# Block 1's key, value and query products in other places, and expert routing written as two generators

## The chip, the cores and the metric

One core of a Trainium2 chip runs the kernel. The metric is the time of one execution on the device in microseconds (us), and lower is better. The engines are TensorE (PE in the profile, with its weight loads as PEld), VectorE (DVE), ScalarE (ACT), GpSimd (POOL) and SyncE (SP). Sixteen DMA engines move data; SP issues the plain loads and POOL issues the gathers.

## The reference

The kernel computes two layers of a bidirectional encoder over 256 tokens with 1024 features. Cut to what matters, a layer is:

```python
h = rms_norm(x, attn_norm)
qa, ka, va, qb, kb, vb, qc, kc, vc = split(h @ w_in)     # three groups of heads of 64
q, k = rope(rms_norm(q)), rope(rms_norm(k))
o = softmax(q k^T + mask) v                              # full, dilated and windowed heads
x = x + (concat(rms(oA), rms(oB), rms(oC)) * out_norm) @ w_out
h = rms_norm(x, ffn_norm)
s = (h @ wq) against keys                                # 8 heads x 2 halves x 128 keys
sv, si = top_k(s, 16); best, pos = top_k(sv[0] + sv[1], 16)
idx = si[0][pos] * 128 + si[1][pos]; gate = softmax(best)
act = gelu(h . u[idx]) * gate                            # 128 experts for each token
x = x + sum_k act_k * v[idx_k]
```

Each token so picks 8 x 16 = 128 experts of 16384. A row of `u` and the row of `v` beside it make 8 KB for one token.

## The kernel before, in words

The 256 tokens are two blocks of 128, block 0 and block 1, with one token on each of the 128 partitions. Everything is 32-bit float. The program is written out in full by Python generators: each generator issues instructions and yields, and the order in which they are stepped is the order of the instructions on every engine.

A layer has a short part before the gather and a long part with it.

**Before the gather.** Block 1's keys and values come from `proj_kv(l, 1)`, which takes its columns in three pieces (`KCH`): 512 columns of keys, 256 columns of keys and values, and 512 columns of values. The two key pieces are followed by `qk_rope`, some 30 VectorE instructions. `keys_t` transposes the keys. Then `attn(l, 0, filler)` runs block 0's attention through `chain_idle`, where four pairs of heads go through `scores`, `softmax`, `divide`, `values` (transposing the weights) and `pv`, and `product` and `add` apply W_out. `chain_idle` steps a generator `filler` at one place, to put TensorE work between two waits. Before the change the filler is the third piece of `proj_kv(l, 1)`, called `values1`; its eight products with 512 columns are all issued there. Then block 0's expert routing begins: `route` makes one item of one or two heads (`HEADS`), in the order query product (`rq`), copy (`q2`), key scores (`rs`), copy (`sS`), the search for the best sixteen on VectorE (`top16`), the expert numbers (`EF`, `EI`), and the gate. While head 0 is routed, `mixer_in` and `proj_q(l, 1)` (block 1's queries, sixteen products with 512 columns) are stepped beside it. When head 0's numbers are there, POOL's gathers may begin; head 1 is routed to its end before the loop over gathered rows.

**The loop.** There are 256 rows n for a layer, 128 for each block. Row n of the loop is one expert for each of 128 tokens: `fetch` gathers 128 x 8 KB (1 MB) by one indirect DMA on POOL's queue, `dots` multiplies and sums on VectorE, `weigh` makes a diagonal matrix on ScalarE (Gelu, times the gate, times the identity), and `gather_up` adds the row to two PSUM banks by TensorE. A row lives in one of 16 slabs of 8 KB per partition, which it shares with the weights in use (w_out and wq hold eight of them while block 1's attention and routing are still to come), so that eight rows are under way at a time at first.

Between rows the loop steps two lanes, `rq` (routing) and `bg` (block 1's query rotation, attention and `mixer_in`, later the next layer's first products). What a step issues is counted by `Meter`: for VectorE 0.15 us and one us for 960 columns of each instruction, for TensorE four us for 2400 columns. Each row adds `DVE_SHARE` = 1.05 and `PE_SHARE` = 0.75 us of credit, up to `SAVED`:

```python
dq, pq = min(dq + DVE_SHARE, SAVED), min(pq + PE_SHARE, SAVED)
while dq > -0.5 and pq > -1.5:
```

Routing takes a step only while `dq` is above 0, and `bg` only while `pq` is. A step that yields n is not taken up again before n rows later. A row's gather needs the expert numbers of its head (16 rows a head), so the loop forces routing when it is late:

```python
while routed() < min((n + 3) // 16 + 1, 16):
    if not rq.step():
        bg.step()
```

Block 1's routing is opened when block 0's routing and block 1's attention are both through, or at row 112. PSUM has two banks for the accumulators and six for all else (`NPS`); `take` and `give` count them.

Of the kernel before, what the change touches and what calls it, by code (L numbers as in the profile page):

```python
# [8 lines left out]
F32 = mybir.dt.float32  # L9
# [11 lines left out]
NPS = 6  # L21
DVE_SHARE = 1.05
PE_SHARE = 0.75
SAVED = 0.8
LEAD = 30
EPS = 1e-6
NKV = 1280
# [32 lines left out]
def tile_trunk(ctx: ExitStack, tc: tile.TileContext, x, wkv, wq_in, w_out, wq, keys, uv0, uv1,  # L60
               cons, qkg, sinks, gains, out):
    nc = tc.nc
# [104 lines left out]
    def take(n):  # L167
        while room[0] < n:
            yield 1
        room[0] -= n  # L170
# [182 lines left out]
    def attn(l, b, filler=None):  # L353
# [53 lines left out]
        def divide(g):  # L407
            P = PR[g]
            ls, es = SM[g]
            if es is not None:  # L410
                dve.tensor_tensor(out=ls, in0=ls, in1=es, op=OP.add)
            dve.reciprocal(ls, ls)
            if idle:
                dve.tensor_tensor(out=P, in0=P, in1=ls.unsqueeze(2).to_broadcast([128, 4, 256]), op=OP.mult)
            else:
                for j in range(4):
                    nc.scalar.activation(P[:, j, :], P[:, j, :], AF.Copy, scale=ls[:, j:j + 1])  # L417
# [14 lines left out]
        def pv(g):  # L432
            hds = []
            for i in range(2):
                kind, hd = pair_info(2 * g + i)
                hds += [(h % 2, 3 * kind + h // 2, vh, 2 * i + s) for s, (h, vh) in enumerate(hd)]
            lo = [a for a in hds if a[0] == 0]
            hi = [a for a in hds if a[0] == 1]
            for pair in zip(lo, hi):
                for t in range(2):  # L440
                    for o, mt, vh, j in pair:
                        pe.matmul(mix[mt // 4][o * 64:o * 64 + 64, mt % 4, :], V[:, t, vh * 64:(vh + 1) * 64],
                                         PTT[g][:, t, j, :], start=(t == 0), stop=(t == 1),
                                         skip_group_check=True)
# [29 lines left out]
        def product(g, z):  # L474

            m0, m1 = GROUPS[g]
            p = ps(f"wo{l}{b}{g}{z}")
            for m in range(m0, m1):
                pe.matmul(p, mT[:, m, :], w_o(l, m, z), start=(m == m0), stop=(m == m1 - 1))
            return p  # L480
# [40 lines left out]
        def chain_idle():  # L521
            scores(0)
            softmax(0)
            scores(1)
            softmax(1)
            divide(0)
            steps(filler, 4)
            rest(keys_t(l, 1, 4, 5))
            rest(filler)
            rest(values(0))  # L530
            scores(2)
            divide(1)
            softmax(2)
            pv(0)
            rest(values(1))
            scores(3)
            divide(2)
            softmax(3)
            pv(1)
            rest(values(2))  # L540
            leave(0)
            divide(3)
            p0 = [product(0, z) for z in range(2)]
            rest(norm_sum(0))
            for z in range(2):
                add(0, z, p0[z])
            pv(2)
            rest(values(3))
            leave(1)
            p1 = [product(1, 0)]  # L550
            rest(norm_sum(1))
            pv(3)
            leave(2)
            p1.append(product(1, 1))
            for z in range(2):
                add(1, z, p1[z])
            rest(norm_sum(2))
            for z in range(2):
                add(2, z, product(2, z))
# [24 lines left out]
        yield from transposes(H2T[l, b].rearrange("p k t -> p (k t)"), 8, ev, f"h2p{l}{b}")  # L584


    BEST, EF, EI, DOT, DONE, GATE, ACT = {}, {}, {}, {}, {}, {}, {}

    def route_alloc(l, b):
        BEST[l, b] = sp.tile([128, 8, 16], F32, tag="best", name=f"best{l}{b}")  # L590
# [18 lines left out]
            dve.max_index(out=idx[:, 8:16], in_max=val[:, 8:16], in_values=scr)  # L609
        yield 0  # L610

    def route(l, b, h0, n):

        nm = f"{l}{b}{h0}"
        yield from take(1)
        pq = ps(f"rq{nm}")
        for hh in range(n):
# [6 lines left out]
        give(1)  # L624
        nc.scalar.activation(q2[:, :n * 128], pq[:, :n * 128], AF.Copy)  # L625
        yield from take(2)
        sS = sp.tile([128, 2, 256], F32, tag="sS", name=f"sS{nm}", bufs=1)
        pk = [ps(f"rs{nm}{p}") for p in range(2)]
        for hh in range(n):
            for p in range(2):  # L630
# [3 lines left out]
        give(2)  # L634
        for p in range(2):
            nc.scalar.activation(sS[:, p, :n * 128], pk[p][:, :n * 128], AF.Copy, scale=RF[l, b][:, 0:1])  # L636
        yield 1
        val = sp.tile([128, 2, 2, 16], F32, tag="rval", name=f"rv{nm}")[:, :, :n]
        idx = sp.tile([128, 2, 2, 16], U32, tag="ridx", name=f"ri{nm}")[:, :, :n]
        scr = sp.tile([128, 2, 128], F32, tag="rscr", name=f"rscr{nm}", bufs=1)  # L640
# [60 lines left out]
        dve.reciprocal(s, s)  # L701
        dve.tensor_tensor(out=g, in0=g, in1=s.unsqueeze(2).to_broadcast([128, n, 16]), op=OP.mult)
        GATED.setdefault((l, b), set()).update(range(h0, h0 + n))
        yield 0

    GATED = {}
# [16 lines left out]

    def weigh(l, b, s):

        a = ACT[l, b][:, s:s + 1]
        nc.scalar.activation(a, DOT[l, b][:, s:s + 1], AF.Gelu)  # L727
        nc.scalar.activation(a, a, AF.Copy, scale=GATE[l, b].rearrange("p h k -> p (h k)")[:, s:s + 1])  # L728
        d = DG[l, b, s] = sp.tile([128, 128], F32, tag="dg", name=f"dg{l}{b}{s}", bufs=4)
        nc.scalar.activation(d, ident, AF.Copy, scale=a)  # L730
# [13 lines left out]

    def open_block(l, b):
        DOT[l, b] = sp.tile([128, 128], F32, tag="dot", name=f"dot{l}{b}")
        ACT[l, b] = sp.tile([128, 128], F32, tag="act", name=f"act{l}{b}")


    uv_rows = (uv0, uv1)  # L750
# [9 lines left out]
    def steps(gen, n):  # L760
        for _ in range(n):
            if next(gen, None) is None:
                return

    def rest(gen):
        for _ in gen:
            pass
# [63 lines left out]
    for l in range(L):  # L831
        if l:
            rest(norm_h(l, 1))
        load(w_out, WO, l, "wo", range(4))
        rest(proj_kv(l, 1, KCH[:2]))
        if l == 0:
            rest(queries_t(0, 0))
        rest(keys_t(l, 1, 0, 4))
        values1 = proj_kv(l, 1, KCH[2:])
        rest(attn(l, 0, values1))  # L840
        load(wq, WQ, l, "wq", range(4))
        open_block(l, 0)
        route_alloc(l, 0)
        rq = Lane(*[route(l, 0, *h) for h in HEADS])

        def routed():
            return sum(len(GATED.get((l, b), ())) for b in range(2))

        hm = mixer_in(l, 0)
        pq1 = proj_q(l, 1)  # L850
        while 0 not in DONE.get((l, 0), ()):
            rq.step()
            steps(hm, 1)
            steps(pq1, 1)
        rest(hm)
        fetch(l, 0, 0)
        rest(pq1)
        finish(rq, until=lambda: routed() > 1)
        bg = Lane(rope_q(l, 1), queries_t(l, 1), attn(l, 1), mixer_in(l, 1))
        dq = pq = 0.0  # L860
        for n in range(256):
            b, s = n // 128, n % 128
            if s == 0:
                ACC[l, b] = [bank(f"acc{z}", f"acc{l}{b}{z}") for z in range(2)]

            dq, pq = min(dq + DVE_SHARE, SAVED), min(pq + PE_SHARE, SAVED)
            while dq > -0.5 and pq > -1.5:
                d, p = dve.spent, pe.spent
                late = routed() < min((n + LEAD) // 16 + 1, 16)
                lanes = (rq, bg) if late or rq.spent < bg.spent else (bg, rq)  # L870
                moved = next((x for x in lanes if (dq if x is rq else pq) > 0 and x.step(n)), None)
                if moved is None:
                    break
                d, p = dve.spent - d, pe.spent - p
                dq, pq = dq - d, pq - p
                moved.spent = max(moved.spent + d + p, max(rq.spent, bg.spent) - 4)
            if (l, 1) not in BEST and not (bg.left or rq.left) or n == 112 and (l, 1) not in BEST:
                finish(bg, rq)
                route_alloc(l, 1)
                open_block(l, 1)  # L880
                rq = Lane(*[route(l, 1, *h) for h in HEADS])
            while routed() < min((n + 3) // 16 + 1, 16):
                if not rq.step():
                    bg.step()
            if n == 132 and l + 1 < L:
                finish(bg)
                load_small(l + 1)
                load(wkv, WKV, l + 1, "wkv", range(5))
                bg = Lane(rope_tables(l + 1), norm_h(l + 1, 0), proj_kv(l + 1, 0), keys_t(l + 1, 0, 0, 4),
                          keys_t(l + 1, 0, 4, 5), once(load, wq_in, WQI, l + 1, "wqi", range(4)),  # L890
                          once(load_late, l + 1), proj_q(l + 1, 0), rope_q(l + 1, 0), queries_t(l + 1, 0))
            if n:
                fetch(l, b, s)
            dots(l, b, s)
            if n == 129:
                settle(l, 0)
            weigh(l, b, s)
            gather_up(l, b, s)
        finish(bg)
        settle(l, 1)  # L900
# [92 lines left out]
```

## Time and profile before

| what | us |
|---|---|
| median of 3 runs | 1558.68 |
| lowest and highest run | 1555.74, 1562.99 |
| the profiled execution, its own time | 1560.36 |
| its span, first to last instruction | 1558.6 |
| TensorE busy in it | 1319.9 |
| VectorE busy | 1036.2 |
| ScalarE busy | 681.5 |
| POOL busy (issuing gathers) | 619.3 |

Times in the rows are microseconds from the start of the span unless ns stands beside them. A matmul of 32-bit floats shows as two instructions. L55 is the line of the meter's helper, so that many operations of TensorE and VectorE have that line, and the tiles' names tell them apart.

### The profile page before, as it was taken

The numbers are of one execution on the slowest core, as the hardware profiler recorded it, in microseconds if no ns is written. First come the engines' busy times: TensorE is split into PE (matmuls) and PEld (weight loads), VectorE is DVE, ScalarE is ACT, GpSimd is POOL, SyncE is SP. The second block draws the span as 40 slices with busy tenths as digits, with TensorE's granted clock in tenths as the row PEclk, the third lists the DMA queues.
The fourth block names the chain that finished last, engine by engine and source line by source line (L and its number), as shares of the span: only waits on it lengthen the run. The fifth ranks groups of instructions, "written<-read, shape, count | busy, mean of one in ns | idle before, by whom it ended". The sixth has DMA issues, their size and how long they took to land. (4 is left out here: it accounts for less than half of the span.)

```text
span 1558.6 us, 15351 instructions
## 1 busy us (share of the span) xinstructions
PE 1319.9 (85%) x3860; PEld 591.2 (38%) x3860; DVE 1036.2 (66%) x3014; ACT 681.5 (44%) x2056; POOL 619.3 (40%) x516
## 2 busy tenths in 40 slices
PE   8896898998868898889878968989998788887777
PEld 4453353443323344433324534444333333332222
DVE  5667868685658777666536587786756767785444
ACT  1323657443434444444323236565434454444333
POOL 0004444555434443423410044545455455555551
PEclk9898999999998999999988989999999999999999
DMA  9308999999999999899991099999999999999996
GB/s 375 156 1 354 420 405 378 395 420 421 419 422 420 421 421 420 343 420 421 422 411 55 17 372 422 414 401 394 421 422 421 422 421 421 422 421 421 422 421 273
DMA packets 81592, 578.62 MB, mean 371 GB/s; under 512 B 9569, under 2 KB 9697, under 8 KB 11873
## 3 DMA queue, kind: packets, MB, share of 16 engines
q0 software_dynamic: 73728, 536.90, 83.6%
q1 hardware_dynamic: 7776, 40.74, 6.5%
q8 instruction: 32, 0.52, 0.1%
q14 instruction: 56, 0.45, 0.1%
HBM read 576.56 MB, written 1.05 MB: 371 GB/s over the span
## 5 line engine op out<-in xcount | busy, mean ns | idle before, releaser
L735 PE MATMUL acc<-uv,dg 128*128 128x512 f32 x2048 | 999.9, 622 | 208.6 <-ACT dg L730 199.5
L714 POOL DMA_INDIRECT uv<-in_uv_dram,ei x512 | 619.1, 1209 | 913.4 <-PE acc L735 309.1
L719 DVE SCALAR_TENSOR_TENSOR uv<-uv,h 128x1024 f32<-128x1024 f32 x512 | 623.8, 1223 | 345.2 <-DMA uv<-in_uv_dram,ei 331.2
L735 PEld LDWEIGHTS acc<-uv,dg 128*128 128x128 f32 x2048 | 367.3, 193 | 768.8 <-ACT dg L730 445.2
L727 ACT ACTIVATE act<-dot 128x1 f32<-128x1 f32 x512 | 102.9, 201 | 542.0 <-DVE uv L719 541.3
L730 ACT ACTIVATE dg<-CI,act 128x128 f32<-128x128 f32 x512 | 205.5, 401 | 16.7
L728 ACT ACTIVATE act<-act,gate 128x1 f32<-128x1 f32 x512 | 150.8, 295 | 16.7
L55 PE MATMUL pkv<-wkv,hT 128*128 128x512 f32 (+1 forms) x192 | 76.0, 545 | 0.7 <-DVE hT L55 0.7
L55 PEld LDWEIGHTS rq<-h2T,wq 128*128 128x128 f32 x512 | 60.8, 192 | 10.6 <-issue 10.0
L55 PE MATMUL wo<-wo,mT 128*128 128x512 f32 x128 | 58.9, 598 | 5.4 <-DVE mT L55 5.4
L55 PE MATMUL rq<-h2T,wq 128*128 128x128 f32 x512 | 61.6, 276 | 0.0
L55 PE MATMUL pq<-wqi,hT 128*128 128x512 f32 x128 | 58.4, 592 | 0.0
L55 DVE MAX8 rv<-sS 128x8 f32<-128x128 f32 x64 | 17.3, 290 | 53.4 <-ACT sS L636 52.9
L55 PEld LDWEIGHTS pkv<-wkv,hT 128*128 128x128 f32 x192 | 37.9, 201 | 37.3 <-issue 34.4
L719 DVE DVE_READ_ACCUMULATOR uv<-uv,h 128x1 f32 x512 | 42.5, 83 | 0.0
L55 PEld LDWEIGHTS wo<-wo,mT 128*128 128x128 f32 x128 | 23.7, 190 | 33.4 <-issue 30.6
L727 ACT ACT_TABLE_LOAD x28 | 35.9, 1283 | 0.5
L55 PEld LDWEIGHTS pq<-wqi,hT 128*128 128x128 f32 x128 | 24.0, 190 | 28.7 <-issue 28.5
L636 ACT ACTIVATE sS<-rs,f_r 128x128 f32<-128x128 f32 (+1 forms) x48 | 16.7, 399 | 41.4 <-PE rs L55 41.4
L55 DVE TENSOR_REDUCE ef<-eq 128x16 f32<-128x512 bf16 x32 | 34.3, 1072 | 0.5
L625 ACT ACTIVATE q<-rq 128x128 f32<-128x128 f32 (+1 forms) x24 | 7.5, 312 | 59.4 <-PE rq L55 59.4
L429 ACT ACTIVATE PT<-pt 128x512 f32<-128x512 f32 x32 | 17.6, 589 | 34.2 <-PE pt L55 34.2
(163 smaller groups left out, 792.4 us busy)
## 6 DMA issues: line engine op xcount, KB each, us to landing
wkv<-in_wkv_dram SPq DMA_DIRECT2D x8, 1024.0 KB, 13.4
wqi<-in_wqi_dram SPq DMA_DIRECT2D x8, 1024.0 KB, 15.2
wo<-in_w_out_dram SPq DMA_DIRECT2D x8, 1024.0 KB, 14.0
wq<-in_wq_dram SPq DMA_DIRECT2D x8, 1024.0 KB, 10.9
uv<-in_uv_dram,ei POOLq DMA_INDIRECT x512, 16.5
wkv<-in_wkv_dram SPq DMA_DIRECT2D x4, 512.0 KB, 6.3
X<-in_x_dram SPq DMA_DIRECT2D x2, 512.0 KB, 6.2
KEYS<-in_keys_dram SPq DMA_DIRECT2D x2, 512.0 KB, 19.7
```

The source lines that it names most:

```text
L55: return f(*args, **kw)
L429: nc.scalar.activation(PT[:, t, :, :], p.rearrange("p (j q) -> p j q", j=4), AF.Copy)
L625: nc.scalar.activation(q2[:, :n * 128], pq[:, :n * 128], AF.Copy)
L636: nc.scalar.activation(sS[:, p, :n * 128], pk[p][:, :n * 128], AF.Copy, scale=RF[l, b][:, 0:1])
L714: nc.gpsimd.indirect_dma_start(out=t, out_offset=None, in_=uv_rows[l], in_offset=bass.IndirectOffsetOnAxis(ap=EI[l, b, s // 16][:, s % 16: ...
L719: nc.vector.scalar_tensor_tensor(out=t[:, :1024], in0=t[:, :1024], scalar=1.0, in1=H2[l, b], op0=OP.mult, op1=OP.mult, accum_out=DOT[l, b] ...
L727: nc.scalar.activation(a, DOT[l, b][:, s:s + 1], AF.Gelu)
L728: nc.scalar.activation(a, a, AF.Copy, scale=GATE[l, b].rearrange("p h k -> p (h k)")[:, s:s + 1])
L730: nc.scalar.activation(d, ident, AF.Copy, scale=a)
L735: nc.tensor.matmul(ACC[l, b][h], DG[l, b, s], ROW[l, b, s][:, 1024 + h * 512:1536 + h * 512], start=(s == 0), stop=(s == 127), skip_group_ ...
```

## The change

`proj_kv(l, 1)` is run with all three pieces ahead of the key transposes, so that the value products stand right behind the two key products. `chain_idle`'s filler is now `proj_q(l, 1)`: it is stepped four times where the value products were, and once, once and twice at three further places, eight steps in all, which are eight of its sixteen products. The rest of it stays beside head 0's routing.

`route` becomes two generators for all items of a block, stepped by `side_by_side`: `key_scores` (query product, copies, key scores) and `pick` (all from the search on). `key_scores` of item i waits until item i-2 is picked, and `sS` has two buffers. `SAVED` goes from 0.8 to 1.6. The tile `ACT` goes: the Gelu writes into `DOT`'s own column.

```diff
-SAVED = 0.8
+SAVED = 1.6
...
             steps(filler, 4)
             rest(keys_t(l, 1, 4, 5))
-            rest(filler)
             rest(values(0))
...
             softmax(3)
+            steps(filler, 1)
             pv(1)
             rest(values(2))
             leave(0)
             divide(3)
+            steps(filler, 1)
             p0 = [product(0, z) for z in range(2)]
...
             leave(1)
+            steps(filler, 2)
             p1 = [product(1, 0)]
...
-    def route(l, b, h0, n):
-
+    SCORES, PICKED = {}, set()
+
+    def route(l, b):
+
+        return side_by_side(chain(*[key_scores(l, b, i) for i in range(len(HEADS))]),
+                            chain(*[pick(l, b, i) for i in range(len(HEADS))]))
+
+    def key_scores(l, b, i):
+
+        h0, n = HEADS[i]
         nm = f"{l}{b}{h0}"
+        while i > 1 and (l, b, i - 2) not in PICKED:
+            yield 1
         yield from take(1)
         pq = ps(f"rq{nm}")
...
-        sS = sp.tile([128, 2, 256], F32, tag="sS", name=f"sS{nm}", bufs=1)
+        sS = sp.tile([128, 2, 256], F32, tag="sS", name=f"sS{nm}", bufs=2)
...
+        SCORES[l, b, i] = sS
         yield 1
+
+    def pick(l, b, i):
+
+        h0, n = HEADS[i]
+        nm = f"{l}{b}{h0}"
+        while (l, b, i) not in SCORES:
+            yield 1
+        sS = SCORES[l, b, i]
...
         GATED.setdefault((l, b), set()).update(range(h0, h0 + n))
+        PICKED.add((l, b, i))
         yield 0
...
-        a = ACT[l, b][:, s:s + 1]
-        nc.scalar.activation(a, DOT[l, b][:, s:s + 1], AF.Gelu)
+        a = DOT[l, b][:, s:s + 1]
+        nc.scalar.activation(a, a, AF.Gelu)
...
-        rest(proj_kv(l, 1, KCH[:2]))
+        rest(proj_kv(l, 1))
         if l == 0:
             rest(queries_t(0, 0))
         rest(keys_t(l, 1, 0, 4))
-        values1 = proj_kv(l, 1, KCH[2:])
-        rest(attn(l, 0, values1))
+        pq1 = proj_q(l, 1)
+        rest(attn(l, 0, pq1))
         load(wq, WQ, l, "wq", range(4))
         open_block(l, 0)
         route_alloc(l, 0)
-        rq = Lane(*[route(l, 0, *h) for h in HEADS])
+        rq = Lane(route(l, 0))
...
         hm = mixer_in(l, 0)
-        pq1 = proj_q(l, 1)
         while 0 not in DONE.get((l, 0), ()):
```

## Rows read from the trace of the kernel before

**Rows 1.** The page: gigabytes a second in 40 equal slices of the span.

```profile
GB/s 375 156 1 354 420 405 378 395 420 421 419 422 420 421 421 420 343 420 421 422 411 55 17 372 422 414 401 394 421 422 421 422 421 421 422 421 421 422 421 273
```

**Rows 2.** Stretches; behind the engines' busy times: granted PE clock, DMA share, GB/s.

```profile
60.00:80.00 20.00, 18.34 (x100) 11.16 (x101) 11.69 (x42) 8.96 (x31) 0.00 (x0) 0.86 0.01 2
135.00:160.00 25.00, 21.80 (x45) 8.47 (x46) 21.84 (x58) 10.71 (x38) 11.25 (x10) 0.89 0.92 363
205.00:285.00 80.00, 73.03 (x257) 36.29 (x256) 58.82 (x184) 47.99 (x142) 38.20 (x30) 0.96 0.97 385
285.00:300.00 15.00, 15.00 (x60) 8.70 (x59) 8.39 (x19) 7.57 (x19) 8.05 (x7) 1.00 0.99 389
620.00:640.00 20.00, 15.09 (x44) 7.07 (x43) 13.29 (x33) 8.84 (x24) 9.05 (x8) 0.91 0.68 261
910.00:930.00 20.00, 16.63 (x36) 6.67 (x36) 16.90 (x47) 8.33 (x30) 7.41 (x7) 0.86 0.88 323
985.00:1055.00 70.00, 64.73 (x232) 32.05 (x230) 53.06 (x164) 44.03 (x130) 34.42 (x29) 0.98 1.00 404
1060.00:1070.00 10.00, 10.00 (x47) 6.17 (x45) 5.30 (x11) 4.50 (x12) 7.76 (x7) 1.00 0.93 331
1070.00:1540.00 470.00, 394.79 (x1003) 155.92 (x1001) 308.52 (x795) 203.01 (x633) 240.58 (x186) 1.00 1.01 421
```

**Rows 3.** Timeline of POOL: start, duration, and in brackets the idle time and its end.

```profile
892.28 0.94 POOL L714 DMA_INDIRECT uv<-in_uv_dram,ei  x1 [99.29 <-issue]
...
915.33 0.94 POOL L714 DMA_INDIRECT uv<-in_uv_dram,ei  x1 [13.42 <-PE acc L735]
```

**Rows 4.** Timeline of POOL in layer 0, block 1: the gather of row 192.

```profile
628.81 0.94 POOL L714 DMA_INDIRECT uv<-in_uv_dram,ei  x1 [18.93 <-DVE gs L55]
```

**Rows 5.** Timeline of layer 1 before its gather: products, transposes, scores of block 0.

```profile
819.17 10.91 PE L55 MATMUL pkv<-wkv,hT 128*128 128x512 f32 x32
...
834.50 1.09 PE L55 MATMUL kT<-CI,kraw 128*128 128x128 f32 x4 [4.41 <-DVE kraw L55]
...
836.27 3.78 PE L55 MATMUL sc<-KT,QT 64*128 64x256 f32 x16 [0.69 <-ACT KT L306]
...
839.99 7.32 PE L55 MATMUL pkv<-wkv,hT 128*128 128x512 f32 x16
...
842.22 1.23 DVE L55 TENSOR_TENSOR P<-P,l 128x1024 f32<-128x1024 f32 x1
...
847.25 1.04 PE L55 MATMUL pt<-CI,P 128*128 128x128 f32 x8
...
848.20 1.09 ACT L429 ACTIVATE PT<-pt 128x512 f32<-128x512 f32 x2
```

**Rows 6.** Timeline of PE in layer 0 before its gather, the same place.

```profile
41.48 10.49 PE L55 MATMUL pkv<-wkv,hT 128*128 128x512 f32 x32
52.34 1.06 PE L55 MATMUL qT<-CI,qraw 128*128 128x128 f32 x8 [0.38 <-DVE qraw L55]
...
64.04 7.87 PE L55 MATMUL pkv<-wkv,hT 128*128 128x512 f32 x16
...
71.86 1.04 PE L55 MATMUL pt<-CI,P 128*128 128x128 f32 x8
```

**Rows 7.** Timeline of layer 1: block 1's queries, head 1's scores, the first dot products.

```profile
883.57 13.04 PE L55 MATMUL pq<-wqi,hT 128*128 128x512 f32 x30
...
899.74 0.56 DVE L55 MAX8 rv<-sS 128x8 f32<-128x128 f32 x2 [1.70 <-ACT sS L636]
...
908.53 1.22 DVE L719 SCALAR_TENSOR_TENSOR uv<-uv,h 128x1024 f32<-128x1024 f32 x1
```

**Rows 8.** Stretches, VectorE's dot products alone: busy us, instructions (two a row).

```profile
117.00:624.60 507.60, 231.37 (x378) 0.96 1.00 409
1243.71:1274.46 30.75, 14.77 (x25) 1.00 1.01 421
```

**Rows 9.** Lines: the gathered rows' products; busy us, mean ns, idle time before them.

```profile
L735 PE MATMUL acc<-uv,dg 128*128 128x512 f32 x2048 | 999.9, 622 | 208.6 <-ACT dg L730 199.5
```

More of the change, by code (lines that the diff above doesn't have):

```diff
@@ L584, in mixer_in @@
         yield from transposes(H2T[l, b].rearrange("p k t -> p (k t)"), 8, ev, f"h2p{l}{b}")
-    BEST, EF, EI, DOT, DONE, GATE, ACT = {}, {}, {}, {}, {}, {}, {}
+    BEST, EF, EI, DOT, DONE, GATE = {}, {}, {}, {}, {}, {}
     def route_alloc(l, b):
@@ L746, in open_block @@
         DOT[l, b] = sp.tile([128, 128], F32, tag="dot", name=f"dot{l}{b}")
-        ACT[l, b] = sp.tile([128, 128], F32, tag="act", name=f"act{l}{b}")
     uv_rows = (uv0, uv1)
@@ L880, in tile_trunk @@
                 open_block(l, 1)
-                rq = Lane(*[route(l, 1, *h) for h in HEADS])
+                rq = Lane(route(l, 1))
             while routed() < min((n + 3) // 16 + 1, 16):
```

## Prediction

> **What bounds the kernel now.** I read the page's slices first. Outside three places the memory moves 420 GB/s or so: the kernel is a stream of 512 gathered megabytes, and the engines work beside it. The low places are the start, the slices of 55, 17 and 372 at the change of layer, and a few dips [rows 1]. The second view is the stretches: from 1070 to 1540 us it is 421 GB/s throughout, and what a stretch falls below that is time lost for good, (421 - GB/s) / 421 of its length [rows 2]. The losses with the gather running are:
>
> 135 to 160 us: 58/421 x 25 = 3.4 us. 205 to 285: 36/421 x 80 = 6.8. 285 to 300: 32/421 x 15 = 1.1. 620 to 640: 160/421 x 20 = 7.6. In layer 1, 910 to 930: 98/421 x 20 = 4.7. 985 to 1055: 17/421 x 70 = 2.8. 1060 to 1070: 90/421 x 10 = 2.1 [rows 2]. In all 28.5 us.
>
> Third, POOL's timeline says what ends each hole. The ninth gather of layer 1 came 13.42 us after the eighth, when the first row's products were done and its slab was free [rows 3]. The gather of row 192 in layer 0 waited 18.93 us for VectorE: the numbers of its head were not there [rows 4]. So the time can shrink in three ways: the first gather of a layer earlier, its first slabs given back earlier, or no head late. Engine time saved under a full stream is worth nothing.
>
> **The change part by part.** *The value products.* They are sixteen instructions, with one copy by ScalarE and no DMA. In layer 1 they took 7.32 us behind the scores, and the weights of the first heads, divided at 842.22 + 1.23 = 843.45, were not transposed before 847.25 [rows 5]. Moved up, they begin when the key products end, 819.17 + 10.91 = 830.1, and end at 837.4. That is later than the 834.50 at which the key transposes began, so the scores now wait for them: they came 836.27 - 834.50 = 1.8 us behind those transposes and now begin at 839.2. From the scores' start to the divided weights VectorE and ScalarE need 843.45 - 836.27 = 7.2 us: 846.4. TensorE has scores for 3.78 us and four query products, eight instructions of 13.04/30 = 0.43 us [rows 7], up to 846.4, and one transpose of keys, 0.2. The weights are transposed at 846.6 and not 847.25: 0.6 us.
>
> In layer 0 the key products end at 41.48 + 10.49 = 52.0, the values then end at 59.3, the query transposes (1.06, which stood at 52.34) at 60.4, and by the same steps the scores begin at 62.1, the weights are divided at 69.3 and transposed at 69.6 and not 71.86 [rows 6]: 2.3 us. There the products had taken 7.87 us against layer 1's 7.32, with a granted clock of 0.86 over 60 to 80 us [rows 2], that is partly at 1.2 GHz, after an idle stretch. I take 7.32, since the move closes that stretch. The Trainium skill, TensorE: Matmul & The Clock Gate, "What you observe", has the slow clock as the idle default that activity releases; by 7.87 in place of 7.32 the 2.3 would be 1.8. The trace agrees, as far as 0.86 goes. Bounds for both layers together: 0, if the transposes queue behind the products, and 5, if the copy of the values, which now no longer stands before the transposed weights' copies on ScalarE [rows 5], is all gained. I take 2.9.
>
> *The other four query steps* are four products of 0.86 us, in three places where TensorE waits for the W_out inputs; I cost them at nothing, and at 3.4 us a layer if none were covered. SP's loads of wq are issued after the attention as before, and slabs come free no later.
>
> *Head 1.* Its scores stood behind 15 query products, 13.04 us; its search on VectorE began at 899.74, and the dots of row 0 only at 908.53, behind that search [rows 7]. Now seven products remain, 6.1 us, so TensorE is free 7.0 us sooner. What is late next is head 0's own end on VectorE and its gate on ScalarE, so I take 6.5: dots at 902.0, and the ninth gather 6.5 us sooner against the first, at about 908.8. The first eight rows last the stream 8 x 1.05 MB / 421 GB/s = 19.9 us at least from the first gather's issue at 892.28 [rows 3], so up to 912.2. The ninth then comes before they are through, and the hole closes: 4.7 us in layer 1, 3.4 in layer 0 with the same pattern, of 8.1 in all I take 7.5. Lower bound 4.
>
> *The generators and SAVED.* A step that yields 0 lets `side_by_side` go on with the same generator, and `pick` yields other than 0 only at its gate. So `key_scores` of the next head is not issued during a search but at its gate: one row of the loop sooner, not a search sooner. The second `sS` is idle mostly. SAVED counts for more. Where routing is alone, one head's VectorE work by the meter is 10 searches of 128 (0.28), 5 of 112 (0.27), 3 operations on 512 (0.68) and small ones, 8.8 us, at 1.05 a row some eight rows; four more rows pass in its steps that yield 1, where credit above 0.8 is lost. That is twelve rows a head, as the trace shows: 25 instructions, two a row, in 30.75 us [rows 8]. Now three rows pass, and 1.6 is kept: (8.8 - 1.6)/1.05 + 3 = ten rows.
>
> I counted the loop's credits in this manner, row by row, for both versions. For the kernel before, the count has block 1's heads 4 and 5 forced at row 189; the trace has 378 instructions, 189 rows, up to there [rows 8]. For the change it has them at rows 164 and 166, with block 1's routing opened at row 95 and not 110. Row 192's gather then waits for nothing: of 7.6 us I take 7.5, lower bound 5. Block 0's heads 4 and 5 move from rows 60 and 61 to 54 and 57; row 64's gather is wanted near row 58, since eight rows are under way. Of the 1.1 and 2.1 us lost there I take 2.5, lower bound 0.
>
> What does it cost? In the first 32 rows of a layer the count gives VectorE 31 us of filler in place of 26, TensorE 18 in place of 13. A row costs VectorE 231.37/189 = 1.22 and TensorE 999.9/512 = 1.95 us busy [rows 8, 9] of the 2.49 that its 1.05 MB take, so a mean of 0.97 and 0.56 more just about fits, though not in every row. The attention stretches lost 6.8 and 2.8 us already [rows 2]; I take 1 us more in each, with bounds from all of these 9.6 gained to as much lost again. The Gelu in `DOT` and the tile that goes are as many instructions: nothing.
>
> **Sum.** 2.9 + 7.5 + 7.5 + 2.5 - 2 = 18.4 us. The profiled execution has 1560.36, so 1542.0; against the median of the runs, 1558.68, it is 1540.3. I say 1540.
>
> **The rivals.** *Routing as late as before.* The generators gain one row a head and the credit is eaten by attention; the waits of rows 64 and 192 stay. Against it stands the count. What is left is 2.9 + 7.5: 1548.
>
> *The attention stretches gain too.* The slabs come back earlier and the stream enters these stretches full, so that their 9.6 us and the 2 go: 1529. For it speaks that layer 1 lost 2.8 us where layer 0 with the same instructions lost 6.8.
>
> *Filler in the way, the other side.* TensorE runs in order, so a row's products stand behind filler that waits for ScalarE; 199.5 us of its idle time before rows' products end with ScalarE [rows 9]. With twice the credit more filler stands in one row. In rows 24 to 31 the count has TensorE's filler at 1.07 us a row; beside four instructions of the size of rows 7, 0.43 each, that is 2.79, 0.3 above the stream's 2.49. If the first 64 rows of both layers went at that pace they would lose 38 us, and the gains are 20.4: it decides from about 68 of these 128 rows on. All of them: 1558.7 - 20.4 + 38 = 1576.
>
> *A bank held.* The query product keeps one of six PSUM tiles through the whole attention chain. Each transposed group is copied in 1.09 / 2 = 0.55 us [rows 5]; if each of the eight turns waited for one copy, 4.4 us a layer: 1549. In the order of use the chain never needs more than five besides, so I doubt it. The Trainium skill, Perfetto Trace Analysis, "Matmuls", wants independent groups rotated through different banks, so that copies overlap the next group; a bank kept open goes against that, and no row here shows its price.
>
> **How the numbers follow.** My forecast 0.55; attention gains too 0.14; routing late 0.14; bank 0.06; filler in the way 0.11, half of it bad enough to be slower by over 0.5% and half about even. 0.5% is 7.8 us, about what a measurement of this kernel can tell from no change. Faster by more: 0.87; within: 0.08; slower: 0.05. The forecast's own range is 1533 to 1547. The range given reaches from the second rival to 1553: small bounds (0 + 4 + 5 + 0) and the attention stretches 3.3 us worse.
>
> **What would show it.** In the profile after: the scores of block 0 begin later by some 2 to 3 us against the key products, yet the first gathers come 0.6 to 2.5 us earlier; the ninth gather comes 14 to 18 us after the first, not 23; no stretch like 620 to 640 at 261 GB/s; the numbers of block 1's heads 4 and 5 near row 166. I am wrong if the 205 to 285 and 985 to 1055 stretches, moved, lose more than 20 us, or if a new wait of TensorE stands before the scores.

## The result, and the profile after

The changed kernel takes 1544.4 us (median of 6 runs, 1542.4 to 1545.6) and the kernel before beside it 1561.2: a ratio of 0.989, 95% interval 0.986 to 0.991. The profiled execution went from 1560.36 us to 1542.42, its span from 1558.6 to 1540.7: 17.9 us less.

Where the 17.9 came from is worked out from four instants of each trace: in each layer the first gather's issue and the last row's dots. Between them lies the stream, ahead of it the stretch with no gather.

| us | before | after | change |
|---|---|---|---|
| layer 0, to the first gather | 117.06 | 112.85 | -4.2 |
| layer 0, stream | 694.36 | 687.56 | -6.8 |
| layer 1, last dots of layer 0 to the first gather | 80.86 | 77.36 | -3.5 |
| layer 1, stream | 658.23 | 654.82 | -3.4 |
| after the last dots | 8.08 | 8.07 | 0 |

The page's slices, to be read against [rows 1]: the slice of 343 in layer 0 (row 192) is gone, but 396 and 389 stand where 343 and 420 stood, and the change of layer reads 45, 63, 422. New are a 364 in the seventh slice and a 369 in the twenty-sixth.

```profile
GB/s 374 164 5 416 420 410 364 421 418 419 422 421 422 421 421 419 396 389 421 422 405 45 63 422 415 369 411 418 421 422 421 421 421 422 421 421 421 422 421 277
```

Stretches of after, as [rows 2]: the engines' busy time, then granted TensorE clock, DMA share and GB/s.

```profile
205.00:230.00 25.00, 19.66 (x81) 10.76 (x80) 13.79 (x47) 12.29 (x38) 9.21 (x9) 0.99 1.01 423
230.00:245.00 15.00, 13.45 (x36) 6.31 (x35) 14.21 (x55) 12.09 (x35) 6.42 (x6) 0.90 0.74 273
620.00:645.00 25.00, 25.00 (x60) 11.13 (x59) 13.78 (x26) 12.34 (x34) 11.57 (x10) 1.00 0.99 380
665.00:685.00 20.00, 16.91 (x37) 7.02 (x36) 17.35 (x41) 7.43 (x26) 10.69 (x8) 0.91 0.92 357
985.00:1015.00 30.00, 22.16 (x63) 10.22 (x62) 27.98 (x107) 24.22 (x71) 11.91 (x10) 0.94 0.89 350
1010.00:1500.00 490.00, 419.89 (x1090) 175.49 (x1089) 320.67 (x846) 216.75 (x674) 242.41 (x198) 0.98 1.01 421
```

By the prediction's measure, 620 to 645 loses (421 - 380)/421 x 25 = 2.4 us, and 665 to 685 loses 64/421 x 20 = 3.0: row 192's 7.6 us are won only in part, though its gather waits for nothing. 230 to 245 loses 148/421 x 15 = 5.3 us, and 985 to 1015 loses 71/421 x 30 = 5.1: two holes that were not there. They are not lost on top of what was lost before, though. From 75 to 200 us behind the first gather, where the attention of block 1 and the routing of block 0 fill the rows, both layers together lose 13.1 us, and lost 13.1 before; the loss now stands closer together.

Behind row 192, a row of TensorE's work at 620 to 645, and the gather on POOL in the hole of 665 to 685:

```profile
620.82 1.02 PE L55 MATMUL pq<-wqi,hT 128*128 128x512 f32 x2
621.68 1.88 PE L757 MATMUL acc<-uv,dg 128*128 128x512 f32 x4
623.40 1.02 PE L55 MATMUL pq<-wqi,hT 128*128 128x512 f32 x2
...
672.58 2.02 POOL L736 DMA_INDIRECT uv<-in_uv_dram,ei  x1 [5.33 <-PE acc L757]
```

POOL in layer 1, the first gather and the ninth, as [rows 3]: they are 894.15 - 877.77 = 16.4 us apart, and were 23.05.

```profile
877.77 0.94 POOL L736 DMA_INDIRECT uv<-in_uv_dram,ei  x1 [96.10 <-PE rq L55]
...
894.15 1.16 POOL L736 DMA_INDIRECT uv<-in_uv_dram,ei  x1 [6.73 <-PE acc L757]
```

TensorE in layer 1's attention, as [rows 5]. There is no idle time of 4.41 us ahead of the transposes of keys any more, and the sixteen scores take 2.00 us; they took 3.78.

```profile
807.68 17.45 PE L55 MATMUL pkv<-wkv,hT 128*128 128x512 f32 x48
824.98 0.60 PE L55 MATMUL kT<-CI,kraw 128*128 128x128 f32 x4
826.40 2.00 PE L55 MATMUL sc<-KT,QT 64*128 64x256 f32 x16 [0.83 <-ACT KT L306]
828.33 3.70 PE L55 MATMUL pq<-wqi,hT 128*128 128x512 f32 x8
831.87 0.27 PE L55 MATMUL kT<-CI,kraw 128*128 128x128 f32 x1
832.77 1.06 PE L55 MATMUL pt<-CI,P 128*128 128x128 f32 x8 [0.63 <-DVE P L55]
```

What grew is in VectorE's waits (total us, times, longest us). Its search waited 52.9 us for ScalarE's copies of the scores in the kernel before (21 times, the longest 5.5); after:

```profile
DVE uv L741 <- DMA uv<-in_uv_dram,ei: 256.3, 209, 3.7
DVE rv L55 <- ACT sS L648: 113.4, 24, 8.5
```

One such wait, in the timelines of ScalarE, then VectorE, then POOL (start, us, and in brackets the idle time ahead):

```profile
213.43 0.38 ACT L637 ACTIVATE q<-rq 128x256 f32<-128x256 f32 x1 [3.04 <-PE rq L55]
...
219.22 0.84 ACT L648 ACTIVATE sS<-rs,f_r 128x256 f32<-128x256 f32 x2 [4.55 <-PE rs L55]
...
210.55 1.22 DVE L741 SCALAR_TENSOR_TENSOR uv<-uv,h 128x1024 f32<-128x1024 f32 x1 [1.64 <-DMA uv<-in_uv_dram,ei]
...
219.73 0.66 DVE L55 MAX8 rv<-sS 128x8 f32<-128x128 f32 x2 [7.95 <-ACT sS L648]
...
221.21 1.21 DVE L741 SCALAR_TENSOR_TENSOR uv<-uv,h 128x1024 f32<-128x1024 f32 x1
...
225.74 1.26 POOL L736 DMA_INDIRECT uv<-in_uv_dram,ei  x1 [2.50 <-PE acc L757]
233.41 0.94 POOL L736 DMA_INDIRECT uv<-in_uv_dram,ei  x1 [6.41 <-DVE m L55]
```

ScalarE waits for TensorE with both copies, and VectorE for ScalarE: its search stands for 7.95 us with the dots of row 37 behind it, at 221.21, though their data landed at 212.94. Row 38's dots follow at 224.97 and its products end at 233.14. Its slab is the one that row 46 needs, eight rows on: POOL issues that gather at 233.41, 7.7 us after the one before it (the row names another releaser). The hole of 230 to 245 is that.

The search's wait is not the whole of the delay. On TensorE the key scores stand behind three rows' products. And behind row 38's dots ScalarE first makes an attention pair's softmax, from one table load to the next, and TensorE comes to the row's products out of 2.97 us of idle time: they take 3.65 us at a granted clock of 0.54, where row 37's took 1.98. TensorE, then ScalarE, then the stretch of row 38's products:

```profile
213.23 5.32 PE L757 MATMUL acc<-uv,dg 128*128 128x512 f32 x12
218.48 0.71 PE L55 MATMUL rs<-KEYS,q 64*128 64x128 f32 x8
...
223.48 1.98 PE L757 MATMUL acc<-uv,dg 128*128 128x512 f32 x4 [2.38 <-ACT dg L752]
...
229.49 8.79 PE L757 MATMUL acc<-uv,dg 128*128 128x512 f32 x16 [2.97 <-ACT dg L752]
```

```profile
223.44 1.28 ACT L398 ACT_TABLE_LOAD   x1
...
227.18 1.28 ACT L749 ACT_TABLE_LOAD   x1
```

```profile
229.49:233.14 3.65, 3.65 (x5) 1.67 (x6) 3.65 (x17) 3.44 (x13) 0.00 (x0) 0.54 0.52 215
```

### The profile page after: what moved, and what is told of

Same layout as the page of the kernel before. It is cut to its first block, busy times and chain, and to the rows that moved or that the text cites. A ratio compares the mean times of both kernels' runs of the same rounds, so it can differ in the third digit from the quotient of the medians.

```text
span 1540.7 us, 15332 instructions
## 1 busy us (share of the span) xinstructions
PE 1314.3 (85%) x3860; PEld 594.0 (39%) x3860; DVE 1026.5 (67%) x3014; ACT 676.6 (44%) x2052; POOL 594.4 (39%) x516
## 5 line engine op out<-in xcount | busy, mean ns | idle before, releaser
L736 POOL DMA_INDIRECT uv<-in_uv_dram,ei x512 | 594.2, 1161 | 920.3 <-PE acc L757 299.6
L757 PEld LDWEIGHTS acc<-uv,dg 128*128 128x128 f32 x2048 | 374.6, 196 | 764.2 <-ACT dg L752 411.8
L749 ACT ACTIVATE dot<-dot 128x1 f32<-128x1 f32 x512 | 102.9, 201 | 558.9 <-DVE uv L741 558.2
L752 ACT ACTIVATE dg<-CI,dot 128x128 f32<-128x128 f32 x512 | 205.5, 401 | 17.5 <-PE acc L757 0.8
L750 ACT ACTIVATE dot<-dot,gate 128x1 f32<-128x1 f32 x512 | 150.8, 295 | 16.6
L55 DVE MAX8 rv<-sS 128x8 f32<-128x128 f32 x64 | 17.4, 291 | 114.0 <-ACT sS L648 113.4
L55 DVE SCALAR_TENSOR_TENSOR X<-wo,mr_r,X 128x512 f32<-128x512 f32 x24 | 17.8, 748 | 17.5 <-PE wo L55 17.0
```

The costliest lines, as they stand in the source:

```text
L55: return f(*args, **kw)
L736: nc.gpsimd.indirect_dma_start(out=t, out_offset=None, in_=uv_rows[l], in_offset=bass.IndirectOffsetOnAxis(ap=EI[l, b, s // 16][:, s % 16: ...
L749: nc.scalar.activation(a, a, AF.Gelu)
L757: nc.tensor.matmul(ACC[l, b][h], DG[l, b, s], ROW[l, b, s][:, 1024 + h * 512:1536 + h * 512], start=(s == 0), stop=(s == 127), skip_group_ ...
```

## The experiments

The theory: the products moved up give their gain by themselves, through TensorE's clock and an earlier head 1; the routing part wins row 192 and loses about as much, because a search is now issued right behind the copies it waits for. The rivals: the routing carries the gain; or the holes come from twice the credit packing more filler into a row.

| kernel | products | route | SAVED | median | ratio to before, interval | search's wait | lost, 75 to 200 |
|---|---|---|---|---|---|---|---|
| routing_alone | before | generators | 1.6 | 1561.1 | 1.001, 1.000 to 1.003 | 110.2 | 13.7 |
| products_alone | after | before | 0.8 | 1545.3 | 0.990, 0.987 to 0.993 | 52.7 | 12.8 |
| old_route_16 | after | before | 1.6 | 1541.5 | 0.988, 0.986 to 0.990 | 51.2 | 9.5 |
| saved_08 | after | generators | 0.8 | 1546.9 | 0.993, 0.990 to 0.995 | 92.3 | 15.4 |
| after_again | after | generators | 1.6 | 1544.0 | 0.990, 0.988 to 0.991 | 91.4 | 14.3 |
| turn | after | generators, one turn more | 1.6 | 1540.7 | 0.989, 0.986 to 0.991 | 11.6 | 9.8 |
| ahead | after | scores made during the search | 1.6 | 1534.0 | 0.984, 0.981 to 0.986 | 5.6 | 2.1 |
| ahead_08 | after | scores made during the search | 0.8 | 1534.4 | 0.984, 0.981 to 0.986 | 3.1 | 3.9 |
| queries_back | values after, queries before | generators | 1.6 | 1557.3 | 0.998, 0.996 to 0.999 | 101.6 | 12.2 |
| warm_gap | before, four spare ones | before | 0.8 | 1559.3 | 0.999, 0.997 to 1.001 | 51.4 | 12.8 |

The last column but one is the total, in us, that VectorE's search waited for the copies. The last is what the stream loses from 75 to 200 us behind the first gather, both layers together, by the prediction's measure (13.1 in after; after and after_again are one kernel, so a difference of some 1 us says nothing).

**The two halves.** products_alone is the kernel before with these lines (excerpts; the generator `pq1` is made ahead of the attention and no longer behind `mixer_in`):

```diff
-            rest(filler)
...
+            steps(filler, 1)      # in three places: 1, 1 and 2
...
-        rest(proj_kv(l, 1, KCH[:2]))
+        rest(proj_kv(l, 1))
...
-        rest(attn(l, 0, values1))
+        rest(attn(l, 0, pq1))
```

> The kernel before with the product moves alone: all eight groups of block 1's key and value products ahead of its key transposes, its queries as filler in the attention chain; routing one head after the other and SAVED 0.8 stay as they were. Theory (the terms of the two parts add): the first gathers come 4.2 and 3.5 us sooner as in the changed kernel, the scores of block 0 take 2.0 us and not 3.78, the ninth gather of each layer comes some 16 us after the first and not 23; routing's heads stay where they were, so the gather of row 192 in layer 0 is late again by some 15 to 19 us and 7 us are lost there, but no new holes near 230 to 250 and 990 to 1010 us. In all 7.7 + 7 = 14 us below the kernel before, so 1544 to 1549, within 3 us of the changed kernel. Rival (the routing is the larger part): the ninth gather waits as before, and the time is 1551 to 1554.

routing_alone is the rest of the change without them.

> The changed kernel with its product moves undone: the generators and SAVED 1.6 alone. Theory: first gathers at 117 and 892 less what the stream between them gains, scores 3.78 us, ninth gather 22 to 23 us after the first; no wait at row 192 (7.5 us won), but VectorE waits for the scores' copies by ScalarE over 100 us in all, as in the changed kernel and not 53 as before, and 8 to 12 us are lost again in new holes near rows 48 to 64 of each layer. In all 0 to 4 us against the kernel before: 1555 to 1561. Rival (the new holes come from the earlier query products as filler in the attention chain and not from the routing): VectorE's wait stays near 53 us, no new holes, and the time is some 10 us below before: 1548 to 1551.

The products alone give nearly all: 1545.3, with runs from 1537.5 to 1546.9. First gathers are 4.8 and 3.1 us sooner, the streams 5.4 and 2.0 us shorter, and row 192 waits as in [rows 4]:

```profile
598.56 0.94 POOL L716 DMA_INDIRECT uv<-in_uv_dram,ei  x1 [1.06 <-DVE ks_r_r L55]
618.40 0.94 POOL L716 DMA_INDIRECT uv<-in_uv_dram,ei  x1 [18.90 <-DVE gs L55]
```

The routing alone gives nothing: 1561.1, the upper end of what the theory had. Layer 0's stream is only 1.9 us shorter, though row 192 no longer waits, and layer 1's 3.2 longer. A part of that is the ninth gather, 24.1 us behind the first in both layers and not 22 to 23. The time of both fits the theory, and that routing carries the gain is refuted.

**The clock.** warm_gap puts four unused products of the values' size on TensorE behind block 1's key products.

```diff
+        spare = ps(f"spare{l}")
+        for k in range(4):
+            pe.matmul(spare, HT[l, 1][:, k, :], w_kv(l, k, 768, 512), start=(k == 0), stop=(k == 3))
```

> The kernel before with four products of the values' size more, whose result nothing uses, on TensorE between block 1's key products and its key transposes in each layer; nothing is left out. They fill the idle stretch of 4.4 to 5.2 us that stands there before the transposes of the keys. Theory (the scores take 3.78 us because TensorE was idle before them and is granted 1.2 GHz): the scores take 2.0 to 2.3 us, the key transposes 0.6 and not 1.09, and the first gather of each layer comes 1.5 to 2 us sooner; 1556 to 1558, some 3 to 4 us below the kernel before. Rival (the scores are short in the changed kernel because of what is queued beside them, copies and PSUM tiles, not for the clock): 3.78 us as before, first gathers as before or up to 0.5 us later, no change of the time.

TensorE in layer 0, then in layer 1:

```profile
59.83 0.63 PE L55 MATMUL kT<-CI,kraw 128*128 128x128 f32 x4 [2.27 <-DVE kraw L55]
61.14 3.68 PE L55 MATMUL sc<-KT,QT 64*128 64x256 f32 x16 [0.69 <-ACT KT L306]
...
834.94 0.63 PE L55 MATMUL kT<-CI,kraw 128*128 128x128 f32 x4 [0.97 <-DVE kraw L55]
836.26 2.00 PE L55 MATMUL sc<-KT,QT 64*128 64x256 f32 x16 [0.69 <-ACT KT L306]
```

The stretches of the scores, warm_gap in layer 0 and layer 1:

```profile
59.80:64.70 4.90, 4.19 (x20) 3.00 (x20) 4.35 (x23) 0.60 (x1) 0.00 (x0) 0.65 0.00 0
834.90:838.20 3.30, 2.57 (x21) 1.90 (x21) 2.85 (x18) 1.88 (x2) 0.00 (x0) 1.00 0.00 0
```

and of the kernel before in layer 1:

```profile
834.00:840.00 6.00, 4.81 (x21) 3.27 (x21) 5.27 (x25) 1.88 (x2) 0.00 (x0) 0.50 0.00 0
```

The two layers make the test between them. In layer 1 the spare products left 0.97 us of idle time, the granted clock stayed at 1.00 (2.4 GHz), the scores took 2.00 us, and the first gather came 80.86 - 77.93 = 2.9 us sooner. In layer 0 2.27 us stayed idle, the clock was 0.65 over the stretch, the scores took 3.68 us, and the first gather came at 116.98 and not 117.06. With 4.41 us idle, before, it was 0.50 (1.2 GHz) and 3.78 us. The rival (copies and tiles, not the clock) falls, since their order is that of before. The theory had both layers sooner and 1556 to 1558; with one layer won the median is 1559.3, and 2.9 us can't be told from nothing there.

**The query products.** queries_back takes them out of the attention and leaves the values moved.

```diff
-        pq1 = proj_q(l, 1)
-        rest(attn(l, 0, pq1))
+        rest(attn(l, 0, iter(())))
...
+        pq1 = proj_q(l, 1)      # behind mixer_in, as before
```

> The changed kernel with block 1's query products taken back out of block 0's attention: all of them beside the routing again, as before. Value products, generators and SAVED as changed. Theory (the query products between the scores of heads 0 and 1 make the ninth gather late): the first gathers come as in the changed kernel within 1 us, the ninth comes 22 to 24 us after the first and not 16.4, and 6 to 9 us are lost by that: 1549 to 1554. Rival (the ninth gather's 6 us are made up later, since the stream of slabs is held by VectorE behind row 48 anyway): 1544 to 1547.

13.2 us slower than after_again, above the theory's 6 to 9 and outside its range. The ninth gather comes 24.0 and 24.2 us after the first, and the streams are 4.6 and 6.1 us longer. The first gathers are 1.0 and 1.8 later too, for TensorE now idles 4.11 us while VectorE and ScalarE make the softmax, and comes back at the slow clock. The timeline, then the stretch's granted clock (the third figure from the end):

```profile
838.77 1.94 PE L55 MATMUL pt<-CI,P 128*128 128x128 f32 x8 [4.11 <-DVE P L55]
840.64 2.08 PE L55 MATMUL sc<-KT,QT 64*128 64x256 f32 x8
```

```profile
838.70:842.60 3.90, 3.83 (x16) 2.75 (x16) 1.40 (x2) 1.70 (x5) 0.00 (x0) 0.50 0.02 4
```

After has 1.06 and 1.14 us for these two. So the query products pay twice: head 1's scores come sooner, and TensorE doesn't go idle.

**The credit or the order.** Three runs beside each other:

> The changed kernel once more, unedited, beside the three that follow, so that a few us between them can be told. Both theories: 1542 to 1546.

> The changed kernel with SAVED 0.8 in place of 1.6: product moves and generators as they are. By the count of credits block 0's heads 4 and 5 come at rows 58 and 60 and block 1's at rows 178 and 180, in time for the gather of row 192. Theory (the new holes come from the order of the two generators: the search is issued right behind the copies that it waits for): VectorE's wait for the scores' copies stays above 95 us, the holes near rows 48 to 64 stay, 1542 to 1548. Rival (the holes come from twice the credit, which packs more filler into a row): the holes shrink to under 4 of 10 us, 1535 to 1540.

> The kernel before with the product moves and SAVED 1.6: routing is one head after the other as before, with a turn of the loop between a head's scores and its search. By the count block 0's heads 4 and 5 come at rows 56 and 59, block 1's at rows 170 and 176. Theory (order of the generators, not the credit): VectorE's wait for the scores' copies is near 53 us, no new holes near rows 48 to 64, the gather of row 192 waits for nothing: 1535 to 1541, 4 to 9 us below the changed kernel. Rival (the credit of 1.6 makes the holes): holes as in the changed kernel, 1543 to 1548.

With the old order 1.6 is better than 0.8 (1541.5 against 1545.3, in different sets of runs), as row 192 no longer waits and less is lost from 75 to 200 us. With the generators' order the search waits 92.3 us at 0.8, a little under the theory's 95, and 91.4 at 1.6 (and 22.5 more that this profile puts down to issue, 113.4 in the first profile of after); the times are 1546.9 and 1544.0. The holes themselves did what the rival said: at 0.8 the two stretches lose 0.9 and 1.4 us and not 10.

```profile
230.00:245.00 15.00, 14.22 (x49) 6.58 (x48) 14.79 (x57) 12.35 (x35) 5.95 (x5) 0.89 1.01 397
985.00:1015.00 30.00, 25.56 (x100) 12.71 (x98) 21.37 (x80) 18.70 (x55) 13.08 (x12) 1.00 0.99 402
```

But the time did not follow, for over the whole 75 to 200 us saved_08 loses 15.4 us and after_again 14.3: the smaller credit spreads the loss out. So the credit shapes the holes and doesn't make the loss. The order costs 2.6 us of median at 1.6 (4.1 of span; 14.3 against 9.5 in the last column). That is less than the theory's 4 to 9, and 1541.5 lies just above its range. From 955 to 1015 us the old order at 1.6 still loses 4.4 us where after_again loses 6.9: a part of the holes has another cause.

**One turn between scores and search.**

```diff
         while (l, b, i) not in SCORES:
             yield 1
+        yield 1
         sS = SCORES[l, b, i]
```

> The changed kernel with one line more: a head's search lets one turn of the loop pass after its scores are there, so that a row's dots stand on VectorE between the copies of the scores and the search that reads them, as they did before the change. Generators, SAVED 1.6 and product moves as changed. Theory (the missing turn makes VectorE wait and the holes): the wait for the scores' copies falls from 113 to 40 to 65 us, row 80 is reached some 212 us after the first gather and not 215, the holes near rows 48 to 64 shrink by a third to a half as with the old route at the same SAVED (1541.5), and the time is 1537 to 1543. Rival (the generators cost by something else, say the products of the next head ahead of a row's): the wait falls, the time stays at 1543 to 1546.

The wait fell to 11.6 us, well below the 40 to 65 expected, and the time to 1540.7, 3.3 us below after_again in another set of runs. Against the kernel before beside each, it is 19.7 us and after_again 17.9, and the two intervals overlap: one line is worth some 2 to 3 us, at the edge of what these runs can tell, though the last column has 9.8 for 14.3. But holes of 4.5 and 4.0 us stay at 220 to 240 and 985 to 1005. ScalarE there, in order of time:

```profile
208.73 0.40 ACT L753 ACTIVATE dg<-CI,dot 128x128 f32<-128x128 f32 x1
212.61 0.84 ACT L648 ACTIVATE sS<-rs,f_r 128x256 f32<-128x256 f32 x2 [3.47 <-PE rs L55]
213.47 1.28 ACT L398 ACT_TABLE_LOAD   x1
...
216.85 1.28 ACT L750 ACT_TABLE_LOAD   x1
...
218.71 0.40 ACT L753 ACTIVATE dg<-CI,dot 128x128 f32<-128x128 f32 x1
```

From 208.73 to 218.71 ScalarE makes no row's weights: it waits 3.47 us for the scores' products, copies, and makes an attention pair's softmax between two table loads. The dots of rows 36 to 39 began meanwhile, at 209.70 to 217.22, so it is now ScalarE's queue that holds the rows. That this is the whole of what stays is read from the trace, not tried by itself.

**Scores made during the search.** ahead steps the scores in every third step of the search as well as at its turns:

```diff
-        return side_by_side(chain(*[key_scores(l, b, i) for i in range(len(HEADS))]),
-                            chain(*[pick(l, b, i) for i in range(len(HEADS))]))
+        ahead = chain(*[key_scores(l, b, i) for i in range(len(HEADS))])
+        for k, n in enumerate(chain(*[pick(l, b, i) for i in range(len(HEADS))])):
+            if n or k % 3 == 0:
+                next(ahead, None)
+            yield n
```

> The changed kernel, with the two generators of routing stepped otherwise: the scores of the next head get one step in every third step of the search and one at each of its turns, so that they are issued during the search of the head before and stand ready when it ends. All else, SAVED included, as in the changed kernel. Theory (VectorE's wait for the scores' copies, 113 us in 24 places, makes the new holes of the changed kernel): that wait falls below 20 us, the holes near 230 to 250 and 990 to 1010 us lose under half of their 10 us, and the time is 5 to 10 us below the changed kernel, 1534 to 1540. Rival (the volume of filler makes the holes, whoever waits): the wait falls but the holes stay, and the time is within 3 us of the changed kernel, or above it, since each head is now over sooner and more filler is packed in the same rows.

> The kernel that makes the next head's scores during the search (1534.0), with SAVED 0.8 in place of 1.6. Theory (with scores that stand ready the credit matters little, since no head is late and VectorE doesn't wait): 1532 to 1537, VectorE's wait for the scores' copies under 15 us, rows 192 and 64 not late. Rival (the larger credit is what carries it, by finishing heads sooner): the heads come 5 to 15 rows later, a row waits for its numbers again, 1540 to 1546.

1534.0 and 1534.4, the best here, as the theory had it in each: 10 us below the changed kernel by the medians, 8 to 10 by the gains over the kernel before beside each. The same stretches of ahead: no hole at 230 to 245 or 985 to 1015, and 2.1 us lost from 75 to 200 where after_again loses 14.3.

```profile
230.00:245.00 15.00, 15.00 (x58) 7.19 (x58) 12.70 (x45) 14.29 (x39) 8.05 (x7) 1.00 1.02 421
...
985.00:1015.00 30.00, 27.44 (x111) 13.50 (x110) 24.75 (x83) 25.53 (x68) 14.54 (x14) 1.00 1.01 422
```

The scores now stand apart from the search, so ScalarE's wait for their products and VectorE's wait for the copies don't fall in one row. Heads end sooner as well: block 1's heads 4 and 5 of layer 0 have their numbers at rows 149 and 151, and at 164 and 166 in the changed kernel. How much of the gain each gives isn't separated; turn puts some 2 to 3 us on VectorE's wait.

## Why the prediction was right, and where it was not

The range and the sign held, and 1540 was 4 us low, but two sizes were wrong by about 5 us each, with opposite signs.

- **The value products and the attention: 2.9 forecast, 7.7 measured**, above the term's bound of 5. Nearly all of it is there at the point that the forecast priced, the first transposed weights: in layer 1 they come 25.1 us behind the start of the key products and came 28.1, in layer 0 26.0 and 30.4, so 3.0 + 4.4 = 7.4 us sooner where 0.6 + 2.3 was forecast. The step that failed is "TensorE has scores for 3.78 us": that duration was taken from a stretch behind 4.41 us of idle time, and the move fills that idle time. At a granted clock of 1.00 in place of 0.50 the scores took 2.00, the key transposes 0.60, not 1.09, and the value products 17.45 - 10.91 = 6.5 in layer 1, not 7.32. So the scores began later against the key products, as said, but by (826.40 - 807.68) - (836.27 - 819.17) = 1.6 us in layer 1 and not 2.9, and from their start to the transposed weights 6.4 us passed, not the 846.6 - 839.2 = 7.4 forecast. The prediction weighed the clock for the value products and not for what stands behind them. The Trainium skill, TensorE: Matmul & The Clock Gate, "What's actually happening", has the slow clock as the default that activity releases. The trace agrees for these scores as well: 0.50 behind the idle time, 1.00 without it. The query steps, costed at nothing, are worth something here too: without them, in queries_back, the first gathers come 1.0 and 1.8 us later. TensorE in layer 0 after, to be read against [rows 6]:

```profile
41.73 17.35 PE L55 MATMUL pkv<-wkv,hT 128*128 128x512 f32 x48
...
67.70 1.06 PE L55 MATMUL pt<-CI,P 128*128 128x128 f32 x8 [0.63 <-DVE P L55]
```

- **Head 1: 7.5 forecast, 7.5 measured.** The ninth gather was put 16.5 us behind the first and came 16.4 behind it in both layers. In products_alone, where routing is as before, the two streams are 5.4 + 2.0 = 7.5 us shorter. queries_back, with the generators, lost 10.7 us of stream by undoing it.
- **The credit count** was right to the row in layer 0: heads 4 and 5 at rows 54 and 57, and at 164 and 166 in block 1. Row 192's gather waits for nothing, as said.
- **Rows 192 and 64 and the earlier filler: 10.0 - 2 = 8.0 forecast, 2.8 measured.** From products_alone to after the streams shrink by 688.94 - 687.56 = 1.4 and 656.19 - 654.82 = 1.4. Two steps failed.
  - The step "of 7.6 us I take 7.5" took the late head for all that holds these rows. From 500 to 580 us behind the first gather layer 0 lost 7.4 us in products_alone and still loses 5.1 in after, 2.1 in after_again and 3.0 in old_route_16. From 620 to 645 TensorE is busy for 25.00 of 25 us: two instructions of the next layer's query products and a row's four take 623.40 - 620.82 = 2.58 us a row, above the stream's 2.49. Behind that POOL waits for a row's products, 5.33 us ahead of the gather at 672.58.
  - The step "a mean of 0.97 and 0.56 more just about fits, though not in every row" costed busy time, and the cost is a wait. Row 64's gather no longer waits (0.78 us, before 4.12 and 5.24) and is issued 10.3 and 8.2 us sooner against the first, but its dots come 3.2 and 3.5 us later. From 75 to 200 us the stream loses 13.1 us (14.3 in after_again) and products_alone 12.8, though the same credit with the old order has it at 9.5. The prediction saw that `side_by_side` issues the scores at the gate. It did not ask what then stands between the scores' copies and the search, where before a row's dots stood: nothing.
- **The rivals.** Routing late fell with the count. Filler in the way is what happened in small: by TensorE's busy time from 620 to 645, and from 205 to 245 by waits of VectorE and ScalarE. No new wait of TensorE stood ahead of the scores (0.83 us, before 0.69), so the held bank cost nothing that shows there.

Summed: 7.7 + (6.8 + 3.4) = 17.9 against 2.9 + 15.5 = 18.4. The sum was right by cancellation, and that was luck.

## What to carry to other kernels

When a move fills an engine's idle stretch, price again the matmuls behind it: here sixteen of them took nearly half the time, and the term came out at more than twice its forecast. When two generators are joined, write down what stands on each engine's queue between a producer and its consumer; a consumer issued right behind its producer's copy makes all behind it wait, and one row's turn was worth 2 to 3 us here, real lookahead 8 to 10. When a late item is mended, look at what else holds the rows behind it. When a hole closes, measure the whole stretch around it, for a loss can move without shrinking. And test a change of two parts by halves, for here one half carried nearly all of it.

## What the runs showed of the hardware

Two rather close idle times of TensorE ahead of the same sixteen scores went two ways in one execution: 0.97 us left them at a granted clock of 1.00 and 2.00 us, 2.27 us had 0.65 over the stretch and 3.68 us. The two places differ in more than that, for in layer 0 eight query transposes stand between the spare products and the idle time. In the stream, too, a row's products behind 2.97 us of idle time had 0.54 and took 3.65 us, where the row before had taken 1.98.
